# Hybrid decoder layer in seven-product blocks: last block's differences, a left-over product, two row loads and some copies moved in the order

## The chip, the cores and the metric

The kernel runs on one core of a Trainium2 chip. The metric is the device time of one launch in microseconds (us), as the median of several runs. The core has five engines that run side by side and wait for each other by semaphores: TensorE (PE, matrix products, with PEld for loading its weights), VectorE (DVE, elementwise work), ScalarE (ACT, activations and copies), GpSimd (POOL) and SyncE (SP, which issues most DMA transfers). Each engine works off its own instructions strictly in the order in which the program lists them.

## The reference

```python
xn = rms_norm(h, ln_g)
proj = jnp.einsum('bsd,de->bse', xn, w_in)
b_gate, c_gate, x_conv, g_conv, x_lru, g_lru = jnp.split(proj, splits, axis=-1)
y_conv = b_gate * causal_depthwise_conv(c_gate * x_conv, conv_w)
y_conv = headwise_rms_norm(y_conv, 8, conv_out_g) * jax.nn.silu(g_conv)
y_lru = rg_lru_mixer(x_lru, lru_conv_w, ...)
y_lru = headwise_rms_norm(y_lru, 16, lru_out_g) * jax.nn.silu(g_lru)
y = jnp.concatenate([y_conv, y_lru], axis=-1)
h = h + jnp.einsum('bse,ed->bsd', y, w_out)
return rms_norm(h, final_g)
```

All is float32, with 2048 positions, a model width of 1024 and an input projection to 6144 columns. `rg_lru_mixer` is a width-4 convolution `u`, two gates (sigmoids of small block-diagonal products of `u`) and a linear recurrence over positions. Nearly all arithmetic is in the two large projections.

## The kernel before

**The steps.** The program is a list of 64 steps (`steps`, L268 to L272), written out in an order that is fixed by hand; no scheduler changes it. Steps 0 to 23 compute the input projection for the first 1024 positions, one step for each 256 columns: kind `l` (`lru`, L707), `a` (`conv_a`, L821) and `b` (`conv_b`, L857) in turn. Steps 24 to 47 do the same for the second 1024 positions. Steps 48 to 55 and 56 to 63 are the output projection (kind `o`, `outp`, L884).

**A step.** A step multiplies a 2x2 set of weight blocks (the stationary side, tiles `s`) with a 2x2 set of activation blocks (`T`, tiles `th` and `tl`). From step 3 on it does so with seven block products instead of eight: products 0 to 6 use sums and differences of the blocks, and their results are added up in four PSUM banks A to D. Each operand is split into a rounded high part and the rest (`th` and `tl`; the two halves of an `s` tile), so a product is 4 blocks x 3 matmuls of 128x512, 12 in all (`mm`, L1009). Sums, splits and copies lie on DVE (line 163 for all elementwise additions and differences), ACT (casts to the high part at L213 for weights, L451, L1160 and L1221 for activations) and POOL.

**The order within a step.** A step runs through slots (loop at L1261). Usually these are products 0, then product 6 of the step before (left over from it), 1, 3, 2, 4, 5. Bank A gathers products 0, 1, 2 and 5, and after each of the first three ACT copies the partial sum out (`q1` at L1315, `u2` at L1318, `rr` at L1321); the next product on bank A must wait until that copy has read it. Those copies are named `q`, `u` or `rr` in the profile, whichever tile they alternate to: line L1318 is always the copy after product 1, L1321 the one after product 2. Bank B may take product 6 only when the combination before (`xx`, `ob`, `gb` or `gl` from the bank, by `put(22, ...)`) has read it.

**Helpers.** `at(k, f)` runs `f` at the k-th `tick`, that is, k slots later. `prep(n, s)` is a step's piece of preparation: from step 3 to 23 it forms and splits weight tiles (`s_plan`, L192: `hi(i)` is ACT's cast, `lo(i)` the rest on DVE or POOL), later it loads ready tiles from DRAM (`s_loads`, L236). `defer` holds a function back while `held[0]` is a list, and `release` runs what was held.

**Changes of the activation set.** The activations change at steps 24, 48 and 56. These steps open the new set with eight products on what is ready (L1240), the next one (25, 49, 57) is `late` and runs products 0, 4, 5, 1, 3, 2 (`AFTER`, L233); their product 6 comes in the step after. A `Change` object loads, subtracts and splits the new blocks in numbered slots: `of_x` (L478) for the positions, `of_w` (L500) for the output weights, `cut` (L447) for casts and low parts.

**The plain start.** Steps 0 to 2 use eight plain products, and beside them the differences of the activation blocks are formed: `bit(j)` (L1155) has four pieces for block j, `do_bits(n)` runs the next n, and `after1` (L1194) and `after2` (L1213) call it in the eight slots of steps 1 and 2. The gates of step 0 (`gates`, L743: four matmuls at L751 into two PSUM tiles; `sigs`, L754: four sigmoids at L758) are due in the slots of step 2. There are two such PSUM tiles, so the second pair of gates waits for the sigmoids of the first.

**Output rows.** The second half of the output projection needs rows that an earlier step left in DRAM (`od`), loaded by `load` (L891) into `xr`, and added at L942 (`ob<-ob,xr`). SP issues its transfers one after the other, the loads of `s`, `tl`, `raw` and `zr` among them.

## Time and profile before

| what | value |
|---|---|
| median of three runs | 1316.51 us (1314.1 to 1317.4) |
| the profiled execution's own time | 1314.92 us |
| its span | 1313.1 us |
| busy: PE, PEld, DVE, ACT, POOL | 1289.5, 1061.0, 1046.0, 748.7, 250.0 us |
| mean granted clock of PE | 0.996 |
| DMA | 355.29 MB, mean 271 GB/s |

The span lies between the first and the last instruction of the profiled execution; its own time is 1.8 us longer. A row in order of time has the start in the span, the duration, engine, line, operation and `out<-in`; `[3.41 <-ACT i L758]` means that the engine idled 3.41 us before it until ACT's operation on `i` at line 758 was done. A row of stretches has the stretch, its length, busy time and number of instructions of each engine, the granted clock of PE as a share of full speed, the share of time in which the DMA engines were busy, and GB/s.

### The profile page before, as it was taken

What the parts mean: (1) busy time and instruction counts of PE and PEld (TensorE: products, weight loads), DVE (VectorE), ACT (ScalarE), POOL (GpSimd) and SP (SyncE); (2) the same over time, 40 slices, a digit from 0 to 9 for tenths busy, and PEclk for the clock granted to TensorE, in tenths of its full rate; (3) what the DMA queues carried; (4) which work ended last, traced back from release to release, by engine and by line L of the source; (5) the groups of instructions that cost most, each with busy time, mean ns of one, the idle gap of its engine ahead of it and who ended that gap; (6) DMA issues with size and microseconds to landing.
All of it is one profiled execution on the core that took longest, in us unless ns stands there. A gap on an engine that the chain in (4) does not pass through costs nothing.

```text
span 1313.1 us, 16711 instructions
## 1 busy us (share of the span) xinstructions
PE 1289.5 (98%) x5688; PEld 1061.0 (81%) x5688; DVE 1046.0 (80%) x1284; ACT 748.7 (57%) x1141; POOL 250.0 (19%) x189
## 2 busy tenths in 40 slices
PE   7989999999999999999999999999999999999997
PEld 6867888888888888778888888888888888887886
DVE  6789898999999998967666666667559767649886
ACT  7576767576675667566454645454466433445443
POOL 3204243344435441001010110101011000000000
PEclk9989999999999999999999999999999999999999
DMA  7128887898989887651899999999789986697654
GB/s 294 32 90 290 290 286 264 302 350 283 345 302 329 295 301 280 207 199 33 277 318 296 340 352 333 324 355 362 236 271 339 260 261 229 249 402 273 235 179 160
DMA packets 157958, 355.29 MB, mean 271 GB/s; under 512 B 16944, under 2 KB 51760, under 8 KB 157872
## 3 DMA queue, kind: packets, MB, share of 16 engines
q1 hardware_dynamic: 153264, 338.17, 74.4%
q0 software_dynamic: 4320, 15.73, 3.1%
q8 instruction: 45, 0.74, 0.2%
q14 instruction: 41, 0.34, 0.1%
q10 hardware_dynamic: 288, 0.32, 0.1%
HBM read 217.11 MB, written 137.04 MB: 270 GB/s over the span
## 4 chain that ended last, share of the span: by engine, by line
PE 82%; DVE 8%; DMA 5%; ACT 3%; issue 2%; SPq 0%; POOL 0%; ACTq 0%; DVEq 0%
PE bank L1014 79%; DMA s<-so 2%; DVE tl L163 2%; PE gate L751 2%; DVE traw L163 1%; DMA tl<-td 1%; DMA zr<-rsd 1%; DMA xr<-od 1%; DMA fg<-in_final_g_dram 1%; DVE u L723 1%; ACT i L758 0%; DVE s L163 0%; ACT r L758 0%; ACT th L451 0%; PE tp L554 0%
## 5 line engine op out<-in xcount | busy, mean ns | idle before, releaser
L1014 PE MATMUL bank<-th,s 128*128 128x512 f32 x3632 | 1129.6, 390 | 5.7 <-ACT rr L1318 1.6
L1014 PEld LDWEIGHTS bank<-th,s 128*128 128x128 f32 x3632 | 682.7, 188 | 151.7 <-ACT rr L1318 2.5
L1014 PE MATMUL bank<-tl,s 128*128 128x512 f32 x1816 | 708.2, 390 | 1.8 <-DVE tl L163 1.6
L1014 PEld LDWEIGHTS bank<-tl,s 128*128 128x128 f32 x1816 | 341.4, 188 | 74.5 <-DVE tl L163 3.0
L163 POOL TENSOR_TENSOR s<-raw,s 128x512 fp32r<-128x512 f32 x62 | 115.1, 1870 | 231.1 <-ACT s L213 176.0
L213 ACT CAST s<-raw 128x512 fp32r<-128x512 f32 x140 | 85.4, 618 | 48.4 <-PE bank L1014 32.8
L163 POOL TENSOR_TENSOR gb<-gb,sg 128x1024 f32<-128x1024 f32 x16 | 43.4, 2712 | 335.5 <-ACT sg L682 335.5
L163 DVE TENSOR_TENSOR s<-raw,s 128x512 fp32r<-128x512 f32 (+1 forms) x125 | 91.6, 755 | 10.6 <-ACT s L1073 6.7
L163 DVE TENSOR_TENSOR s<-s,s 128x512 fp32r<-128x512 f32 x105 | 86.6, 824 | 2.1 <-ACT s L213 1.5
L163 DVE TENSOR_TENSOR tl<-traw,th 128x512 fp32r<-128x512 f32 x85 | 60.8, 748 | 19.4 <-ACT th L451 13.4
L213 ACT CAST s<-s 128x512 fp32r<-128x512 f32 x105 | 64.7, 616 | 4.3 <-DVE s L163 4.0
L723 DVE SCALAR_TENSOR_TENSOR u<-xl,pt,u 128x1024 f32<-128x1024 f32 x48 | 61.3, 1278 | 6.1 <-ACT u L719 5.5
L835 DVE SCALAR_TENSOR_TENSOR t<-p,pt,t 128x1024 f32<-128x1024 f32 x32 | 46.5, 1454 | 16.6 <-ACT t L832 15.8
L1315 ACT COPY q<-bank 128x512 f32<-128x512 f32 x58 | 33.9, 584 | 40.9 <-PE bank L1014 31.5
L163 DVE TENSOR_TENSOR st<-u,st 64x512 fp32r<-64x512 f32 x64 | 53.8, 841 | 2.0
L758 ACT ACTIVATE r<-gate,pt 64x512 f32<-64x512 f32 x64 | 43.7, 683 | 17.3 <-PE gate L751 16.5
L1318 ACT COPY rr<-bank 128x512 f32<-128x512 f32 x31 | 18.1, 584 | 53.6 <-PE bank L1014 53.3
L1318 ACT COPY u<-bank 128x512 f32<-128x512 f32 x27 | 15.8, 585 | 52.4 <-PE bank L1014 52.4
L163 DVE TENSOR_TENSOR traw<-traw 128x512 f32<-128x512 f32 x60 | 41.8, 701 | 4.7 <-DMA traw<-in_w_out_dram 3.6
L451 ACT CAST th<-traw 128x512 fp32r<-128x512 f32 x64 | 36.1, 618 | 16.1 <-DVE traw L163 14.2
L758 ACT ACTIVATE i<-gate,pt 64x512 f32<-64x512 f32 x64 | 43.8, 684 | 1.1
L1321 ACT COPY u<-bank 128x512 f32<-128x512 f32 x31 | 18.1, 585 | 43.6 <-PE bank L1014 43.5
(169 smaller groups left out, 1294.1 us busy)
## 6 DMA issues: line engine op xcount, KB each, us to landing
sd<-s SPq DMA_DIRECT2D x151, 512.0 KB
s<-sd SPq DMA_DIRECT2D x151, 512.0 KB
raw<-in_w_in_dram SPq DMA_DIRECT2D x104, 256.0 KB
raw<-yd SPq DMA_DIRECT2D x64, 256.0 KB
traw<-in_w_out_dram SPq DMA_DIRECT2D x64, 256.0 KB
so<-so SPq DMA_DIRECT2D x22, 512.0 KB
s<-so SPq DMA_DIRECT2D x22, 512.0 KB
yd<-gl SPq DMA_DIRECT2D x32, 256.0 KB
```

What stands on the lines that cost most here:

```text
L163: (eng or nc.vector).tensor_tensor(out=out, in0=a, in1=b, op=op)
L213: nc.scalar.copy(dst[i][0], val(i))
L451: nc.scalar.copy(self.dst[i, j][0], self.r[i, j])
L723: nc.vector.scalar_tensor_tensor(out=v["u"], in0=o1[:, 1 + j:1 + j + N2], scalar=lw[j], in1=v["u"], op0=ALU.mult, op1=ALU.add)
L751: nc.tensor.matmul(ps[j], v["gw"][n][:, j, :], v["st"][j][:, sl], start=(n == 0), stop=(n == 1))
L758: nc.scalar.activation(out=g_[hi, sl], in_=v["ps"][j][src], func=AF.Sigmoid, bias=pt[src, bias + k:bias + k + 1])
L835: nc.vector.scalar_tensor_tensor(out=tcur["t"], in0=p[:, 2 + j:2 + j + N2], scalar=cw[j], in1=tcur["t"], op0=ALU.mult, op1=ALU.add)
L1014: nc.tensor.matmul(bank, a[:, js], b, start=start and n == 0, stop=stop and n == 2, skip_group_check=more)
L1315: nc.scalar.copy(q1, bk["A"])
L1318: nc.scalar.copy(u2, bk["A"])
L1321: nc.scalar.copy(rr, bk["A"])
```

## The change

The edits are small, and each moves instructions; no operation is added or left out.

- Steps 1 and 2: the last four pieces of `bits`, block 3, go from the last two slots of step 1 into the first four slots of step 2, one each.
- Steps 3 to 23, and the later ones that form their weight tiles themselves: `hi(5)` is deferred, and `held[0]` is opened in the slot of product 0, so that ACT's cast of this weight tile (`s2` or `s`) stands behind the copy `q1`.
- Step 25 and 26, at the change of positions: `sixth` does its four subtractions in one slot and the four casts and low parts in the next; step 26 runs products 0, 3, left-over 6, 1, 2, 4, 5; and the scaling `m1` of `conv_a` is held back there until the copy `u2`.
- Steps 49 and 57 (the `late` ones of the output projection): the casts of `Change` in the slot of product 1 come behind the copy `u2`, and the preparation of the next step in the slot of product 2 behind the copy `rr` and the two combinations that use it.
- Step 56: the two row loads three slots sooner.

```diff
-                lambda: hi(5),
+                lambda: defer(lambda: hi(5)),
...
-        def sixth(self, *js):
-            for j in js:
+        def sixth(self):
+            for j in range(NB):
                 tt(self.r[6, j], self.r[6, j], self.r[1, j], ALU.subtract)
-            self.cut([(6, j) for j in js])
+            at(1, lambda: self.cut([(6, j) for j in range(NB)]))
...
-                self.sixth(0, 1)
-                at(1, lambda: self.sixth(2, 3))
+                self.sixth()
...
-                at(1, m1)
+                at(1, lambda: defer(m1))
...
-            at(5, lambda: load(0))
-            at(6, lambda: load(1))
+            sooner = 3 if ph == 1 and m == 2 else 0
+            at(5 - sooner, lambda: load(0))
+            at(6 - sooner, lambda: load(1))
...
-            do_bits(2)
+            if s < 6:
+                do_bits(2)
...
         def after2(s):
-            do_bits(2)
+            do_bits(1)
...
             slots = (0, 6) + ORDER[1:] if not late else AFTER
+            if kind != "o" and n > 1 and opens(n - 2):
+                slots = (0, 3, 6, 1, 2, 4, 5)
...
+                if i == 1 and slots[2] == 6:
+                    held[0] = []
                 tick()
...
                 if late:
-                    change.slot(16 + s)
+                    if i != 1 or kind != "o":
+                        change.slot(16 + s)
...
                 elif s == 0:
+                    held[0] = []
                     prep(n, 6)
...
-                    held[0] = [] if i == 2 else None
-                    prep(n + 1, s - 1)
+                    if i == 2 and not late:
+                        held[0] = []
+                    if i != 2 or kind != "o" or not late:
+                        prep(n + 1, s - 1)
...
-                if s == 1 and not late:
+                if i == 6 and not late and s < 3:
...
                 if i == 0:
                     q1 = sm_q1[0] = sm("q1")
                     nc.scalar.copy(q1, bk["A"])
+                    release()
                 elif i == 1:
                     u2 = sm_u2[0] = sm(("u2", "rr")[n % 2])
                     nc.scalar.copy(u2, bk["A"])
+                    release()
+                    if late and kind == "o":
+                        change.slot(16 + s)
...
                     if late:
                         put(12, bk["D"], rr)
+                        if kind == "o":
+                            prep(n + 1, s - 1)
```

What this does to the engines' orders is shown at three places. A row there is a line of the program it is from (the lines of the changed kernel differ by one or more from those of the profile), the operation, `out<-in` and the size.

On ACT at the border of steps 1 and 2, before (`th<-traw` are the casts of the activation blocks, `s<-raw` of a weight tile, `xx` and `p` copies of PSUM banks, `r` and `i` the sigmoids of step 0's gates):

```order
L1160 CAST th<-traw 128x512
L814 COPY xx<-bank 128x512
L814 COPY p<-bank 128x512
L1160 CAST th<-traw 128x512
L1073 CAST s<-raw 128x512
L1160 CAST th<-traw 128x512
L814 COPY xx<-bank 128x512
L758 ACTIVATE r<-gate,pt 64x512
L758 ACTIVATE i<-gate,pt 64x512
L758 ACTIVATE r<-gate,pt 64x512
L758 ACTIVATE i<-gate,pt 64x512
L832 ACTIVATE t<-p,pt 128x1024
```

And the same place on ACT in the changed kernel:

```order
L1160 CAST th<-traw 128x512
L813 COPY xx<-bank 128x512
L813 COPY p<-bank 128x512
L1073 CAST s<-raw 128x512
L813 COPY xx<-bank 128x512
L757 ACTIVATE r<-gate,pt 64x512
L757 ACTIVATE i<-gate,pt 64x512
L757 ACTIVATE r<-gate,pt 64x512
L757 ACTIVATE i<-gate,pt 64x512
L831 ACTIVATE t<-p,pt 128x1024
L839 COPY hp<-p 128x2
L1160 CAST th<-traw 128x512
```

Two casts have left the place between the copies; the first of them now stands behind `t`, the second behind the four sigmoids that follow it. On DVE the six operations of block 3 have moved along: one goes ahead of the two multiply-adds `t<-p,pt,t` of step 1, five behind them.

On ACT in steps 25 and 26, before (`th<-traw` are the casts of the four blocks for product 6, `u_5065` is the copy `rr` of step 25, `q_5099` and `u_5149` the copies `q1` and `u2` of step 26):

```order
L451 CAST th<-traw 128x512 x2
L1321 COPY u_5065<-bank 128x512
L451 CAST th<-traw 128x512 x2
L1315 COPY q_5099<-bank 128x512
L758 ACTIVATE r<-gate,pt 64x512
L758 ACTIVATE i<-gate,pt 64x512
L758 ACTIVATE r<-gate,pt 64x512
L758 ACTIVATE i<-gate,pt 64x512
L620 CAST rt<-sums 128x512
L832 ACTIVATE t<-p,pt 128x1024
L1318 COPY u_5149<-bank 128x512
```

And the same place on ACT in the changed kernel:

```order
L1334 COPY u_5059<-bank 128x512
L451 CAST th<-traw 128x512 x4
L1324 COPY q_5099<-bank 128x512
L757 ACTIVATE r<-gate,pt 64x512
L757 ACTIVATE i<-gate,pt 64x512
L757 ACTIVATE r<-gate,pt 64x512
L757 ACTIVATE i<-gate,pt 64x512
L619 CAST rt<-sums 128x512
L757 ACTIVATE r<-gate,pt 64x512
L757 ACTIVATE i<-gate,pt 64x512
L757 ACTIVATE r<-gate,pt 64x512
L757 ACTIVATE i<-gate,pt 64x512
```

The copy `rr` of step 25 stands ahead of all four casts, the second group of sigmoids has come forward, and the copy `u2` and the scaling `t` follow behind this piece. On DVE all four differences come ahead of `xx<-bank,u`, and the four low parts behind it. On PE the order of products is 0, 3, 6, 1, 2 instead of 0, 6, 1, 3, 2; the four gate matmuls and the small products of `norm_ps` (L627) keep their slots.

On SP in step 56, before (`fg` are the final gains, `td` the stored differences of the output weights, `od` the rows):

```order
L889 DMA fg<-in_final_g_dram 128x1024
L239 DMA s<-so_125 128x1024
L518 DMA tl<-td_130 128x512
L518 DMA tl<-td_131 128x512
L518 DMA tl<-td_132 128x512
L518 DMA tl<-td_133 128x512
L239 DMA s<-so_125 128x1024
L894 DMA xr<-od_138 128x1024
L239 DMA s<-so_125 128x1024
L307 DMA raw<-yd_86 128x512 x2
L297 DMA zr<-rsd_89 128x1024
```

And the same place on SP in the changed kernel:

```order
L888 DMA fg<-in_final_g_dram 128x1024
L239 DMA s<-so_125 128x1024
L893 DMA xr<-od_138 128x1024
L517 DMA tl<-td_130 128x512
L517 DMA tl<-td_131 128x512
L517 DMA tl<-td_132 128x512
L517 DMA tl<-td_133 128x512
L893 DMA xr<-od_139 128x1024
L239 DMA s<-so_125 128x1024 x2
L307 DMA raw<-yd_86 128x512 x2
L297 DMA zr<-rsd_89 128x1024
```

The first row load has passed four `tl` transfers and one `s`; the second, which stood behind both pairs of `raw` and their `zr`, has passed two `s`, four `raw` and two `zr`.

## The prediction

> **What bounds the kernel now.** I read the page first, then the waits of PE, then PE, ACT and DVE in order of time around each wait. The page says that TensorE (PE) has almost no idle time:
>
> ```profile
> PE 1289.5 (98%) x5688; PEld 1061.0 (81%) x5688; DVE 1046.0 (80%) x1284; ACT 748.7 (57%) x1141; POOL 250.0 (19%) x189
> ```
>
> So the change can only win where PE idles or its clock is low. The stretches of the span (after the span of time: its length, then busy time and instruction count of PE, PEld, DVE, ACT and POOL, the granted clock, DMA share, GB/s) say what kind of place that is:
>
> ```profile
> 50.00:100.00 50.00, 46.31 (x188) 36.68 (x187) 42.44 (x57) 33.56 (x50) 4.48 (x5) 0.93 0.19 66
> 380.20:436.90 56.70, 56.70 (x252) 46.89 (x250) 54.59 (x56) 37.42 (x55) 24.82 (x15) 1.00 0.91 313
> 550.00:650.00 100.00, 97.44 (x428) 79.44 (x427) 71.77 (x85) 60.00 (x82) 9.62 (x5) 1.00 0.49 160
> ```
>
> The second row is one cycle of three steps in the middle: PE has no gap, 252 matmuls in 56.70 us, 0.225 us each, which I use below as the pace of PE at full clock. A product of 12 matmuls is 2.7 us. Nothing that only touches such a cycle can gain. The first and the third hold gaps, and the first a lower clock. The waits of PE over the whole span (sum, times, longest) give the list:
>
> ```profile
> PE gate L751 <- ACT i L758: 3.6, 2, 3.4
> PE bank L1014 <- ACT rr L1318: 1.6, 2, 1.3
> PE bank L1014 <- DVE xx L163: 1.3, 1, 1.3
> PE bank L1014 <- DVE ob L163: 1.1, 1, 1.1
> PE norm_ps L627 <- ACT i L758: 0.8, 1, 0.8
> ```
>
> These five are the four places that the edits touch: the second plain step, step 26, step 49, and steps 57 and 58. Other waits of PE (the start, the end, `q1` in step 3) keep their instruction order.
>
> **Part 1: the last block's differences out of the second plain step.** PE, in order of time (start, duration, in brackets the idle time and what ended it):
>
> ```profile
> 73.25 0.39 PE L1014 MATMUL bank<-th,s 128*128 128x512 f32 x1
> 77.05 0.79 PE L751 MATMUL gate<-st,bh 128*128 128x512 f32 x1 [3.41 <-ACT i L758]
> 78.45 0.79 PE L751 MATMUL gate<-st,bh 128*128 128x512 f32 x1 [0.18 <-ACT i L758]
> 79.47 0.63 PE L1014 MATMUL bank<-th,s 128*128 128x512 f32 x1
> 83.74 0.41 PE L1014 MATMUL bank<-tl,s 128*128 128x512 f32 x1
> ```
>
> The second pair of gate matmuls needs the PSUM tiles of the first pair, which ACT's four sigmoids read. ACT was late:
>
> ```profile
> 70.56 0.59 ACT L814 COPY p<-bank 128x512 f32<-128x512 f32 x1
> 73.17 0.62 ACT L1160 CAST th<-traw 128x512 fp32r<-128x512 f32 x1 [2.02 <-DVE traw L163]
> 74.62 0.62 ACT L1160 CAST th<-traw 128x512 fp32r<-128x512 f32 x1 [0.31 <-DVE traw L163]
> 75.62 0.68 ACT L758 ACTIVATE r<-gate,pt 64x512 f32<-64x512 f32 x1
> ```
>
> Two casts of the last block waited for its differences on DVE, and the sigmoids stood behind them. In the new order both casts stand behind the sigmoids. ACT goes on from 70.56: 0.5 for the copy of `p`, 0.5 for the cast of `s`, 0.5 for the copy of `xx`, so the first sigmoid starts at 72.1 instead of 75.62. From that sigmoid to the gate matmuls it was 1.43 us to the first pair (77.05) and 2.83 to the second (78.45); so they may start at 73.5 and 74.9. PE gets there at 73.5: the 3.41 us are gone, and about 0.8 is left before the second pair. The clock:
>
> ```profile
> 78.00:80.00 2.00, 1.82 (x5) 1.26 (x5) 0.39 (x1) 1.98 (x4) 0.00 (x0) 0.50 0.03 8
> ```
>
> It was 0.50 after the 3.41 us of idling, and the ten matmul intervals from 79.47 to 83.74 took 4.27 us instead of 2.25. The longest idle times elsewhere in the steady program, 1.3 us in the list above, stand in rows with a clock of 1.00, so I take it that 0.8 us leaves the clock alone. Then the second pair starts 3.57 us earlier, the 1.02 us from there to 79.47 become about 0.55 (half the time, rounded up), and the 4.27 become 2.25: 3.57 + 0.47 + 2.02 = **6.1 us**. Bounds: 3.6 if the clock falls all the same, 6.9 if the 0.8 us goes too.
>
> The Trainium skill ("TensorE: Matmul & The Clock Gate", section "A second HAM failure mode: psum-queue depth-cycling") speaks against this: short idle times between groups of matmuls, each far below the window, can be enough to make the clock fall again and again. By it this part gains 3.6 and the whole sum is 2.5 us smaller. The rows with 1.00 around waits of 1.3 us are against it here.
>
> What takes the place: DVE. Of its six moved operations five now follow its pair of multiply-adds, which started at 79.61 when ACT's `t` was ready and now start some 3.5 us earlier:
>
> ```profile
> 79.60:100.80 21.20, 18.12 (x25) 0.90 0.47 171
> 100.09 0.69 DVE L163 TENSOR_TENSOR tl<-t,th 128x512 fp32r<-128x512 f32 x1
> 101.47 0.50 PE L1014 MATMUL bank<-th,s 128*128 128x512 f32 x1 [0.73 <-ACT q L1315]
> ```
>
> From 76.1, with 18.1 us of work and five or six more operations of 0.65 (row 100.09 has 0.69), DVE is through with the last low part at 98.1, only 2.7 us earlier than 100.8, while PE comes 6.1 earlier. So DVE loses 3.4 us of its lead on PE. The low parts of `T[3]` are first read in the product after the one at 101.47, 2.7 us on, so the lead was more than that; I cost the lag at nothing and keep up to 2.7 us as its upper end. The 0.73 us for `q1` stays: in step 3 there is no left-over product between product 0 and product 1.
>
> **Part 2: step 26 and the deferred `m1`.**
>
> ```profile
> 555.48 0.50 PE L1014 MATMUL bank<-th,s 128*128 128x512 f32 x1 [1.32 <-DVE xx L163]
> 557.33 0.50 PE L1014 MATMUL bank<-th,s 128*128 128x512 f32 x1 [0.19 <-ACT th L451]
> 566.70 0.71 PE L627 MATMUL norm_ps<-rt,sel 128*96 128x256 f32 x4 [0.82 <-ACT i L758]
> 567.25 0.39 PE L1014 MATMUL bank<-th,s 128*128 128x512 f32 x1
> 554.01 0.58 ACT L1321 COPY u<-bank 128x512 f32<-128x512 f32 x1
> ```
>
> The left-over product waits for `xx`, which waits for the copy `u`, queued behind two casts on ACT that wait for DVE. Now the casts follow the copy and all four differences stand ahead of `xx`; product 3 runs 2.7 us between. Two differences take the place of two low parts ahead of `xx`, so DVE has it at 555.4 as before, and PE needs it at 556.7. The four low parts behind it end at about 556.4 to 558.3 (0.6 apart, as two of DVE's operations take 1.28 in row 1190.77 below) and are read from 556.9 on, three matmuls (0.68) apart: covered by 0.5 us. The last gate matmul ahead of the wait starts at 555.48 less 1.32 less its own 0.40, 553.76, and PE is free 0.2 later. From there to 567.25 are 13.3 us; three products (8.1), four gate matmuls (0.9) and `norm_ps` (567.25 less 566.70, 0.55) are 9.6, so 3.7 are waits. What comes new: products 1 and 2 follow each other on bank A with the copy between them. A bare copy costs PE 0.9 us (row 101.47: 0.73 and the ramp); 0.55 of it lies under `norm_ps`, some 0.4 us stay. I take **3.3 us**; bounds 2.4 (the copy late by an ACT operation and a half) and 3.7.
>
> **Part 3: step 49.** Two casts move behind the copy that PE waits for.
>
> ```profile
> 1028.02 0.50 PE L1014 MATMUL bank<-th,s 128*128 128x512 f32 x1 [0.33 <-ACT rr L1318]
> ```
>
> The copy comes 1.0 us earlier, two casts of 0.5: the wait goes, with the matmul latency around it **0.6 us** (0.3 to 0.7). The casts are read two products later.
>
> **Part 4: steps 56 to 58, the rows sooner.**
>
> ```profile
> 1161.09 0.32 SPq L894 DMA_DIRECT2D xr<-od  x1
> 1162.36 0.32 SPq L239 DMA_DIRECT2D s<-so  x1
> 1172.86 1.29 DVE L163 TENSOR_TENSOR raw<-raw,zr 128x512 f32<-128x512 f32 x2 [0.29 <-DMA zr<-rsd]
> 1177.08 1.22 DVE L163 TENSOR_TENSOR ob<-ob,xr 128x1024 f32<-128x1024 f32 x1 [2.93 <-DMA xr<-od]
> 1182.74 0.69 DVE L163 TENSOR_TENSOR s<-s,raw 128x512 f32<-128x512 f32 x1
> 1184.05 0.58 ACT L1318 COPY rr<-bank 128x512 f32<-128x512 f32 x1
> 1184.68 0.50 PE L1014 MATMUL bank<-th,s 128*128 128x512 f32 x1 [1.30 <-ACT rr L1318]
> 1190.77 1.28 DVE L163 TENSOR_TENSOR ob<-bank,u 128x512 f32<-128x512 f32 x2
> 1191.51 0.50 PE L1014 MATMUL bank<-th,s 128*128 128x512 f32 x1 [1.05 <-DVE ob L163]
> ```
>
> DVE waits 2.93 us for the second row; what is behind it releases a cast on ACT and the copy that PE needs. With both rows ahead, the next to come last is `zr`. SP passes one 512 KB transfer per 1.27 us here (the two SP rows), and one transfer more is now ahead of `zr`: 1174.1 instead of 1172.86, two multiplications, and `ob` starts at 1175.4, 1.7 us earlier. The copy had ended at 1184.63 and ends at 1182.9 then. PE is free at 1183.2 (1184.68 less the wait and a ramp of 0.2): the wait of 1.30 goes, 1.6 with the ramps. For the left-over product of step 57, DVE reaches `ob<-bank,u` 1.7 us earlier and 1.2 more since two operations now follow it: done at 1188.5 (1190.77 + 0.68 - 2.9), where PE comes after two products at 1183.2 + 5.4 = 1188.6: 1.05 and its ramps, 1.3, go. Together 2.9, less 0.2 for leads this thin: **2.7 us** (1.3 to 2.9). The `s` and `tl` transfers that the rows pass come 1.3 to 2.6 us later; PE's list above names no DMA among its waits, so I cost that at nothing; without that cover it would be up to 2.6 us, the second rival's size.
>
> **Costed at nothing:** the swap of `hi(5)` behind `q1` in the steps between. The cast of 0.62 us moves past a copy; DVE idles 56.70 less 54.59, 2.1 us a cycle, and three casts are 1.9. Without that cover see the third rival.
>
> **The sum:** 6.1 + 3.3 + 0.6 + 2.7 = 12.7 us. The profiled execution took 1314.92 us, its span 1313.1: 1302.2. The median of the three runs, 1316.51, lies 1.6 above it, so I forecast 1303.8 for a median.
>
> **The rivals.** *First: PE catches DVE, or the clock falls.* In step 3 PE waits up to 2.7 us for low parts, or part 1 gains 3.6 instead of 6.1. For: DVE is the busiest engine there after PE. Time: 1303.8 + 2.6 = 1306.4. *Second: the end is not mended*, as the 0.2 to 0.4 us of lead in part 4 are too thin: 1303.8 + 2.7 = 1306.5. *Third, the other side: DVE becomes the bound in the seven cycles of steps 3 to 23.* The three later casts use up 1.9 of its 2.1 us; if they also shift its operations into POOL's, an operation can take this:
>
> ```profile
> 106.67 2.89 DVE L163 TENSOR_TENSOR s<-raw,s 128x512 fp32r<-128x512 f32 x1
> ```
>
> That is 2.2 more than the 0.69 of its kind. With two more such collisions a cycle: 1.9 + 4.4 - 2.1 = 4.2 us by 7, 29 us, 1333; it decides from one a cycle on, 2.0 by 7 = 14 us, which eats the gain. Against: from 150 to 520 DVE waits for PE's banks five times, so it is through in time:
>
> ```profile
> DVE xx L163 <- PE bank L1014: 4.0, 5, 1.0
> ```
>
> By the Trainium skill ("GPSIMD Engine Reference", section "Specifications") VectorE and GpSimd share their SBUF interfaces, and an operation with two SBUF inputs is one of those that suffer. The 2.89 us agree. *Fourth: the DMA gives it back.* Loads bind the stretch from 700 on and do not come earlier, so PE waits for them: 9.4 of the gains lost, 1313.2. Against: in the row from 550 the DMA share is 0.49, so its queue drains there and moves with PE.
>
> **Chances.** Forecast 0.60 (its own range 1301 to 1306), first rival 0.20, second 0.08, fourth 0.05, third 0.04, and 0.03 for more than I count. A measurement of this kernel can tell about 0.3%, 4 us, from no change: the forecast, the first two rivals and the rest are faster, 0.91; the fourth is the same, 0.05; the third slower, 0.04. The range takes in the low end of the forecast and the first two with 2 us: 1300.5 to 1308.5.
>
> **What would show it.** Right: no wait of the gate matmuls over 1 us near 73, a clock of 1.00 from 50 to 100, PE at the 101.47 matmul near 95.3; no `xx` wait in step 26 and a small one for `u2` behind `norm_ps`; no wait for `rr` in steps 49 and 57 nor for `ob` in step 58. Wrong: a clock of 0.50 near 77, new waits of PE in steps 3 to 23, or the sum of PE's gaps less than 9 us smaller.

## The result

The changed kernel takes 1304.99 us (median of 6 runs, 1303.76 to 1307.17) where the kernel before takes 1316.18 (6 runs, 1314.1 to 1317.4). The ratio is 0.9918, with a 95% interval of 0.9906 to 0.9931: about 10.8 us less, 9.1 to 12.4. The profiled execution of the changed kernel took 1304.39 us, its span is 1302.6: 10.5 us less than before in both. The 12.7 us that the prediction added up are just above the interval of the gain.

TensorE's line of the page, the stretches that stood in the prediction (the cycle in the middle comes 5.1 us earlier now), and the waits of TensorE that are new or answer to those listed for before:

```profile
PE 1285.2 (99%) x5688; PEld 1059.1 (81%) x5688; DVE 1042.7 (80%) x1284; ACT 748.1 (57%) x1141; POOL 247.7 (19%) x189
```

```profile
50.00:100.00 50.00, 48.57 (x210) 38.80 (x210) 45.18 (x61) 37.69 (x56) 5.55 (x6) 1.00 0.23 84
375.10:431.80 56.70, 56.70 (x252) 46.89 (x251) 54.05 (x57) 37.39 (x55) 24.35 (x15) 1.00 0.91 312
550.00:650.00 100.00, 99.76 (x441) 82.34 (x440) 73.24 (x87) 60.91 (x83) 9.66 (x5) 1.00 0.51 171
```

```profile
PE bank L1014 <- ACT u L1334: 1.2, 1, 1.2
PE bank L1014 <- ACT q L1324: 0.7, 1, 0.7
PE gate L750 <- ACT i L757: 0.7, 1, 0.7
PE bank L1014 <- ACT rr L1328: 0.5, 1, 0.5
PE bank L1014 <- ACT u L1328: 0.2, 1, 0.2
```

The clock is 1.00 in the first stretch (0.93 before), the waits for `xx` and `ob` are gone, and the first line of the list is new. (Line numbers differ a little: L758 of before is L757 here, and the copies of L1315, L1318 and L1321 are L1324, L1328 and L1334.) To add the places up, I took from the trace every distance between the starts of two matmuls that follow each other, and of those over 0.3 us what goes beyond 0.225. This holds the waits, their ramps (the wider distances of the first matmuls after a wait) and the half clock; I call it TensorE's excess. It is counted from one profile of each kernel. In us:

| place | before | after | gain | forecast |
|---|---|---|---|---|
| gates near 73, clock | 7.66 | 1.60 | 6.1 | 6.1 |
| steps 3 and 4 (90 to 140) | 1.00 | 2.48 | -1.5 | 0 |
| step 26 | 3.56 | 0.41 | 3.15 | 3.3 |
| step 49 | 0.60 | 0.74 | -0.1 | 0.6 |
| steps 57 and 58 | 2.91 | 0.66 | 2.25 | 2.7 |
| start (to 50) | 7.33 | 7.27 | 0.1 | 0 |
| other places | 0.42 | 0 | 0.4 | 0 |
| all | 23.49 | 13.16 | 10.3 | 12.7 |

The spans differ by 0.2 us more than the places, and 0.5 us of the sum (the start and the other places) is not where the edits are.

**The gates.** TensorE and then ScalarE of the changed kernel, in order of time:

```profile
73.07 0.50 PE L750 MATMUL gate<-st,bh 128*128 128x512 f32 x1
74.47 0.50 PE L750 MATMUL gate<-st,bh 128*128 128x512 f32 x1 [0.67 <-ACT i L757]
75.05 0.39 PE L1014 MATMUL bank<-th,s 128*128 128x512 f32 x1
```

```profile
71.16 0.60 ACT L813 COPY xx<-bank 128x512 f32<-128x512 f32 x1
71.64 0.69 ACT L757 ACTIVATE r<-gate,pt 64x512 f32<-64x512 f32 x1
75.59 0.62 ACT L1160 CAST th<-traw 128x512 fp32r<-128x512 f32 x1
```

The sigmoid follows the copy of `xx` at once, the cast stands behind the sigmoids, and the first pair of gate matmuls waits for nothing. The next product starts 0.58 us after the second pair.

**Step 3.** The new wait, on TensorE, and what ScalarE, VectorE and GpSimd did ahead of it:

```profile
107.31 0.50 PE L1014 MATMUL bank<-th,s 128*128 128x512 f32 x1 [1.17 <-ACT u L1334]
```

```profile
105.12 0.62 ACT L213 CAST s<-s 128x512 fp32r<-128x512 f32 x1 [2.48 <-DVE s L163]
105.64 1.05 ACT L572 ACTIVATE xrow<-xrow 128x1024 f32<-128x1024 f32 x1
106.69 0.57 ACT L1334 COPY u<-bank 128x512 f32<-128x512 f32 x1
```

```profile
97.10 2.28 DVE L784 TENSOR_TENSOR_SCAN r<-r,u 128x1024 f32<-128x1024 f32 x1
99.49 2.06 DVE L663 SCALAR_TENSOR_TENSOR gl<-r,pt,gl 128x1024 f32<-128x1024 f32 x1
101.47 2.89 DVE L163 TENSOR_TENSOR s<-raw 128x512 f32<-128x512 f32 x1
104.39 0.69 DVE L163 TENSOR_TENSOR s<-s,raw 128x512 f32<-128x512 f32 x1
```

```profile
98.92 1.55 POOL L163 TENSOR_TENSOR s<-raw,s 128x512 fp32r<-128x512 f32 x1 [20.46 <-ACT s L213]
100.43 3.38 POOL L163 TENSOR_TENSOR gb<-gb,sg 128x1024 f32<-128x1024 f32 x1
```

TensorE needs the bank that ScalarE copies into `u`. The copy stands in ScalarE's queue behind a cast of step 4's `s`, and this cast waits for VectorE's sum of 104.39. VectorE is late: its scan (97.10) starts 2.13 us behind TensorE's product that waits for `q` (94.97). Before, it started 0.77 us ahead of it (100.70 against 101.47):

```profile
100.70 2.29 DVE L785 TENSOR_TENSOR_SCAN r<-r,u 128x1024 f32<-128x1024 f32 x1
```

So 2.9 us of lead are gone, and two operations beside GpSimd's take 2.06 and 2.89 us.

**Step 26, and step 57.** TensorE in step 26; VectorE in step 57:

```profile
558.00 0.64 PE L626 MATMUL norm_ps<-rt,sel 128*96 128x256 f32 x4
558.88 0.50 PE L1014 MATMUL bank<-th,s 128*128 128x512 f32 x1 [0.24 <-ACT u L1328]
```

```profile
1166.18 1.29 DVE L163 TENSOR_TENSOR raw<-raw,zr 128x512 f32<-128x512 f32 x2 [5.11 <-DMA zr<-rsd]
1167.39 1.22 DVE L163 TENSOR_TENSOR ob<-ob,xr 128x1024 f32<-128x1024 f32 x1
```

The bare copy between products 1 and 2 leaves 0.24 us behind `norm_ps`. In step 57 `ob` no longer waits for a row; the last that it stands behind is `zr`.

**Step 49.** ScalarE, then TensorE:

```profile
1016.04 0.62 ACT L451 CAST th<-tl 128x512 fp32r<-128x512 f32 x1 [7.69 <-DMA tl<-td]
1017.38 0.62 ACT L451 CAST th<-tl 128x512 fp32r<-128x512 f32 x1 [0.73 <-DMA tl<-td]
1018.96 0.58 ACT L1328 COPY rr<-bank 128x512 f32<-128x512 f32 x1
```

```profile
1019.58 0.50 PE L1014 MATMUL bank<-th,s 128*128 128x512 f32 x1 [0.47 <-ACT rr L1328]
```

Two of the four casts do stand behind the copy now, but the other two wait for staged blocks that the DMA queue brings, the second until 1017.38.

### The profile page after: what moved, and what is told of

Its sections match the earlier page's. It is cut to its first block, busy times and chain, and to the rows that moved or that the text cites. A ratio compares the mean times of both kernels' runs of the same rounds, so it can differ in the third digit from the quotient of the medians.

```text
span 1302.6 us, 16692 instructions
## 1 busy us (share of the span) xinstructions
PE 1285.2 (99%) x5688; PEld 1059.1 (81%) x5688; DVE 1042.7 (80%) x1284; ACT 748.1 (57%) x1141; POOL 247.7 (19%) x189
## 4 chain that ended last, share of the span: by engine, by line
PE 84%; DMA 4%; DVE 3%; ACT 2%; issue 1%; SPq 0%; DVEq 0%; ACTq 0%
PE bank L1014 82%; PE gate L750 2%; DMA s<-so 2%; DMA tl<-td 1%; DMA zr<-rsd 1%; DVE s L163 1%; DMA raw<-yd 1%; DVE tl L163 0%; DVE ob L163 0%; DVE r L784 0%; ACT th L451 0%; ACT L769 0%; ACT r L769 0%; DVE u L163 0%; DVE raw L163 0%
## 5 line engine op out<-in xcount | busy, mean ns | idle before, releaser
L163 DVE TENSOR_TENSOR s<-raw,s 128x512 fp32r<-128x512 f32 (+1 forms) x125 | 88.3, 729 | 10.6 <-ACT s L1073 6.7
L1324 ACT COPY q<-bank 128x512 f32<-128x512 f32 x58 | 33.9, 585 | 50.2 <-PE bank L1014 48.5
L757 ACT ACTIVATE r<-gate,pt 64x512 f32<-64x512 f32 x64 | 43.7, 683 | 17.8 <-PE gate L750 17.0
L1328 ACT COPY rr<-bank 128x512 f32<-128x512 f32 x31 | 18.1, 584 | 51.1 <-PE bank L1014 51.0
L163 DVE TENSOR_TENSOR raw<-raw,zr 128x512 f32<-128x512 f32 x64 | 41.1, 683 | 7.6 <-DMA zr<-rsd 7.5
L1328 ACT COPY u<-bank 128x512 f32<-128x512 f32 x27 | 15.8, 585 | 52.2 <-PE bank L1014 51.7
L1334 ACT COPY u<-bank 128x512 f32<-128x512 f32 x31 | 18.1, 584 | 47.0 <-PE bank L1014 46.9
L757 ACT ACTIVATE i<-gate,pt 64x512 f32<-64x512 f32 x64 | 43.8, 684 | 1.1
```

What stands on the lines that cost most here:

```text
L163: (eng or nc.vector).tensor_tensor(out=out, in0=a, in1=b, op=op)
L757: nc.scalar.activation(out=g_[hi, sl], in_=v["ps"][j][src], func=AF.Sigmoid, bias=pt[src, bias + k:bias + k + 1])
L1324: nc.scalar.copy(q1, bk["A"])
L1328: nc.scalar.copy(u2, bk["A"])
L1334: nc.scalar.copy(rr, bk["A"])
```

## The experiments

The theory: the four places of the forecast pay separately, and what is missing has two causes: VectorE's lost lead, which TensorE meets in step 3 through ScalarE's queue, and the landing of the staged blocks in step 49. The main rival: the new wait comes from the cast of `hi(5)` that now stands behind `q1`, and the rest is a matter of single profiles. All times below are ratios to the kernel before on the same chip, with 95% intervals.

**Part 1 alone**, in the kernel before:

```diff
-            do_bits(2)
+            if s < 6:
+                do_bits(2)
...
         def after2(s):
-            do_bits(2)
+            do_bits(1)
```

> The kernel before with part 1 alone (the last block's differences later). Theory: the gates and the clock are worth 6.1 us, and because VectorE keeps only part of its lead, the copy u in step 3 stands behind a cast that waits for VectorE and behind a square, so 1.4 us come back there: 4.7 us less than before, about 1311.5, with a wait of TensorE of 1.0 to 1.3 us for ACT's u in step 3, and the waits of steps 26, 49, 57 and 58 as before. Rival: the new wait in step 3 comes from the cast of hi(5), which the full change puts behind q1: then part 1 alone shows no u wait in step 3 and gains 6.1, about 1310.

Measured: 0.997 (0.9959 to 0.9981), 3.9 us less than 1315.26 (2.5 to 5.4). TensorE's wait in step 3 is there, without any change to `hi(5)`:

```profile
107.25 0.50 PE L1014 MATMUL bank<-th,s 128*128 128x512 f32 x1 [1.02 <-ACT u L1322]
```

Beyond the pace of 0.225 us there are 1.61 us at the gates and 2.50 in steps 3 and 4, as in the changed kernel. The rival falls. The 3.9 us and the 1.5 that come back in step 3 make 5.4, somewhat less than the 6.1 of the table.

**Step 26 alone**, in the kernel before: the methods `sixth` and `of_x`, the line of `m1`, the order 0, 3, 6, 1, 2 and the release behind `u2`, as in the diff of the change.

> The kernel before with the reordered step 26 alone (products 0, 3, sixth, 1, 2, the four differences together, m1 and the casts behind the copy). Theory: 3.3 us less than before, about 1313: the waits of 1.3 and 0.2 us in step 26 go and some 0.4 stay between products 1 and 2. Rival: it only pays together with part 1, or the loads of the output stage take it back: within 1 us of before.

Measured: 0.9974 (0.9964 to 0.9984), 3.4 us less (2.1 to 4.7); step 26 keeps 0.41 us. The theory holds. Its profiled execution also has a wait near 720 that no edit touches; TensorE, and a stretch behind it:

```profile
719.89 0.50 PE L1013 MATMUL bank<-th,s 128*128 128x512 f32 x1 [2.19 <-DMA s<-sd]
```

```profile
722.00:724.00 2.00, 2.00 (x6) 1.56 (x5) 0.00 (x0) 0.00 (x0) 0.00 (x0) 0.50 1.13 390
```

**The rows sooner, alone**, in the kernel before:

```diff
-            at(5, lambda: load(0))
-            at(6, lambda: load(1))
+            sooner = 3 if ph == 1 and m == 2 else 0
+            at(5 - sooner, lambda: load(0))
+            at(6 - sooner, lambda: load(1))
```

> The kernel before with only the two output rows of step 56 loaded three slots sooner. Theory: VectorE's wait of 2.9 us for the second row goes, so the rr wait of 1.3 us in step 57 shrinks to 0.2 or less, but the ob wait of step 58 stays at 0.7 to 1.1 us: 1.5 us less than before. Rival: the rows carry the whole of part 4: both waits go, 2.3 to 2.9 us less. Second rival: the transfers that the rows pass are missed, and TensorE shows a new DMA wait there: no gain.

Measured: 0.9987 (0.9978 to 0.9996), 1.7 us less (0.5 to 2.9). In the trace the excess ahead of the `rr` product of step 57 falls from 1.47 to 0.28, and the wait for `ob` in step 58 stays at 1.07. The theory holds; there is no new DMA wait near the passed transfers. Near 720 this profile too has a wait, a shorter one, and the clock stays:

```profile
721.30 0.50 PE L1015 MATMUL bank<-th,s 128*128 128x512 f32 x1 [1.27 <-DMA s<-sd]
```

```profile
722.00:724.00 2.00, 2.00 (x11) 1.64 (x10) 1.17 (x2) 1.69 (x2) 0.00 (x0) 1.00 1.04 379
```

**Copies first, alone**, in the kernel before (steps 49 and 57):

```diff
                 if late:
-                    change.slot(16 + s)
+                    if i != 1 or kind != "o":
+                        change.slot(16 + s)
...
                     nc.scalar.copy(u2, bk["A"])
+                    if late and kind == "o":
+                        change.slot(16 + s)
...
                         put(12, bk["D"], rr)
+                        if kind == "o":
+                            prep(n + 1, s - 1)
```

> The kernel before with only the casts, differences and low parts of steps 49 and 57 put behind the copies and partial sums. Theory (step 49's wait of after is due to the tl transfers, which did not come earlier in step with TensorE): here nothing ahead is faster, the transfers land as early against TensorE as before, and the 0.6 us of step 49 go; the ob wait of step 58 goes too (1.05 us and its ramp), the rr wait of step 57 stays at 1.2 to 1.4: 1.8 us less than before. Rival: the order of the casts has nothing to do with step 49's wait: it stays at 0.3 to 0.6 us here as well, 1.2 us less.

Measured: 0.9988 (0.998 to 0.9997), 1.6 us less (0.4 to 2.6). The wait of step 49 is gone altogether, so is that for `ob`. The wait for `rr` in step 57 is 0.78 us, where 1.2 to 1.4 were expected and 1.30 stood before; its product starts 7.6 us behind the `ob` operation that waits for the row in both, so the row came sooner against TensorE, which this edit does not explain. The trace fits the theory for step 49, but does not show by itself that the order did it: the fourth staged block landed early here (1.03 us in the count of the table further down, at which the old order would not have waited either). The four parts measured alone sum to 10.6 us, against 10.8 for the whole.

**The swap of `hi(5)` alone**, in the kernel before:

```diff
-                lambda: hi(5),
+                lambda: defer(lambda: hi(5)),
...
                 elif s == 0:
+                    held[0] = []
                     prep(n, 6)
...
                     nc.scalar.copy(q1, bk["A"])
+                    release()
```

> The kernel before with only the cast of hi(5) behind the copy q1 in the steps of the cycles. Theory: it moves nothing that TensorE waits for: the same time within 0.1% (1.3 us), no new wait of TensorE from 150 to 520. Rival (VectorE becomes the bound in the seven cycles): from 1.5 us slower on, with waits of TensorE in steps 3 to 23. Second rival: it is a part of the gain: over 1 us faster.

Measured: 1.0006 (0.9997 to 1.0014), and no wait of TensorE from 150 to 520. It costs nothing that this measurement can tell, as forecast.

**Half of part 1**, in the changed kernel:

```diff
-            if s < 6:
+            if s < 7:
                 do_bits(2)
```

> The changed kernel, but the last slot but one of the second plain step keeps its pair of differences and one cast (only the last slot's pair is moved). Theory: one cast stands ahead of the sigmoids and waits for VectorE again, so TensorE waits 1.0 to 2.0 us before the first gates instead of 0; the clock stays at 1.00 afterwards; VectorE comes 1.3 us less late to step 3, so the u wait of 1.2 us there goes to 0.3 or less: about even with the changed kernel (within 1 us). Rival (short idle times are enough for the clock to fall): a granted clock of 0.50 behind the gates and 2 us more than the changed kernel.

Measured: 0.994 (0.9928 to 0.9953), 2.9 and 3.7 us more than the changed kernel in its two measurements (0.9918 and 0.9912); I had expected within 1. The wait in step 3 is gone (0.95 us in steps 3 and 4, as before), but the cast that stays makes TensorE wait 2.49 us where 1.0 to 2.0 were expected, and the clock falls: the rival came true. TensorE, and the stretch behind the gates:

```profile
77.19 0.50 PE L750 MATMUL gate<-st,bh 128*128 128x512 f32 x1 [2.49 <-ACT i L757]
```

```profile
78.00:80.00 2.00, 1.41 (x3) 1.16 (x4) 0.26 (x1) 1.98 (x4) 0.00 (x0) 0.53 0.03 8
```

**The square behind the copy**, in the changed kernel:

```diff
-            at(3, lambda: nc.scalar.activation(out=t, in_=t, func=AF.Square, accum_out=ss[:, b:b + 1]))
+            at(3 + (c == b == 0), lambda: nc.scalar.activation(out=t, in_=t, func=AF.Square, accum_out=ss[:, b:b + 1]))
```

> The changed kernel with ScalarE's first sum of squares (the instruction of 1.05 us ahead of the copy u in step 3) one slot later. Theory: TensorE waits for u in step 3 because ScalarE passes a late cast and then this square before it copies; with the square behind, u ends 1.2 us sooner and the wait falls from 1.2 to 0.2 us or less: 1.1 us less than the changed kernel. Rival (VectorE's lag itself is the bound): the wait moves to the next product or the next partial sum and the time is the same.

Measured: 0.9922 (0.9908 to 0.9935), the time of the changed kernel. Three waits of TensorE stand where one was:

```profile
106.50 0.50 PE L1014 MATMUL bank<-th,s 128*128 128x512 f32 x1 [0.17 <-ACT u L1334]
115.44 0.50 PE L1014 MATMUL bank<-th,s 128*128 128x512 f32 x1 [0.48 <-ACT q L1324]
130.20 0.47 PE L750 MATMUL gate<-st,bh 128*128 128x512 f32 x1 [0.40 <-DVE st L163]
```

Together with the wait for `q` in step 3 they make 2.79 us against 2.48. My theory that the square is what has to go falls; the rival holds: VectorE's lag is the bound, and it comes out at the next place.

**The staged blocks one slot sooner**, in the changed kernel:

```diff
-            if q in (6, 7, 9, 15):
-                self.place((3, 1, 2, 6)[(6, 7, 9, 15).index(q)])
+            if q in (6, 7, 9, 14):
+                self.place((3, 1, 2, 6)[(6, 7, 9, 14).index(q)])
```

> The changed kernel with the four staged blocks of the sixth product in steps 48 and 56 ordered one slot sooner, so ahead of one 512 KB transfer of s. Theory (step 49's wait comes from ScalarE's casts waiting for these blocks): they land 1.3 us sooner and the wait of 0.5 us for rr in step 49 goes: 0.7 us less than the changed kernel. Rival: the wait has another cause on ScalarE or VectorE and stays at 0.5. Second rival: the passed transfer of s is missed, and TensorE or ScalarE waits for it: no gain or slower.

Measured: 0.9923 (0.9909 to 0.9937). In the trace step 49 waits for nothing, and steps 57 and 58 have 0.30 us in place of 0.66. A difference of 1 us is smaller than the interval, and this trace alone does not show the theory: the changed kernel itself waits for nothing in step 49 in its second profile, which comes next.

**The changed kernel, profiled once more:**

> The changed kernel itself, profiled once more. Theory: what TensorE waits for in steps 3 and 26 and at the gates is the same to 0.05 us, while step 49's wait is a matter of when the second staged block lands: the wait is that landing, counted from the first of the norm_ps matmuls, less 0.95 us (0.63 at 1.58, 0.98 at 1.93, none at 0.80 so far). Rival: step 49's wait is fixed by the order and shows 0.5 to 0.7 us again wherever the block lands.

Measured: 0.9912 (0.9898 to 0.9925). Gates, step 3 and step 26 are the same to 0.02 us (1.60, 2.47, 0.41); step 49 waits for nothing. ScalarE there:

```profile
1015.78 1.31 ACT L451 CAST th<-tl 128x512 fp32r<-128x512 f32 x2 [7.03 <-DMA tl<-td]
1018.03 0.58 ACT L1328 COPY rr<-bank 128x512 f32<-128x512 f32 x1
```

The two casts follow each other here. The table shows, in us, when the block that the copy stands behind has landed by the trace, counted from the start of the first of the `norm_ps` matmuls ahead of the wait, and TensorE's excess at the product behind the copy (without the 0.11 us of the matmul after it, which the first table holds too):

| casts ahead of the copy | kernels | landing | excess |
|---|---|---|---|
| four (fourth block) | before; part 1; step 26; rows; swap | 1.76; 2.19; 2.15; 1.67; 2.49 | 0.49; 0.94; 0.89; 0.43; 1.23 |
| two (second block) | changed; again; half; square; copies first | 1.58; 0.26; 1.93; 0.80; -0.32 | 0.63; 0; 0.98; 0; 0 |

The excess is the landing less 1.26 us in the first row, and the landing less 0.95, or nothing, in the second. The theory holds: the order fixes what the copy waits for, and the landing fixes how long. The queue's order around these blocks is the same in all ten, and the landing moves by 0.8 us (first row) and 2.2 (second). Some of that is chance from one execution to the next: the changed kernel itself stands at 1.58 and at 0.26. Whether the blocks also come later because TensorE is earlier can't be told from these. In the kernel with the blocks one slot sooner and the three further down that are built on it, the second block landed at -0.89, 0.10, -0.50 and -1.03, and none of the four waits in step 49. That is what the theory of the sooner blocks expects.

**Four low parts on GpSimd**, in the kernel with the blocks sooner:

```diff
-                    low(v, T[i, j])
+                    low(v, T[i, j], g if i == 6 else None)
```

> The changed kernel with the staged blocks one slot sooner, and with four of the eight low parts that VectorE makes in the third plain step (those of the sixth left matrix, first read in step 4) made by GpSimd. Theory (VectorE's lag behind the six later differences is what TensorE meets in step 3): VectorE has 4 operations of 0.6 us less, 2.4 us, which is the lag of 2.9 us but for 0.5; the u wait of step 3 falls from 1.2 to 0.3 us or less, no new wait at q in step 3 and at the gates of step 4, and step 49 shows none either: 1.5 to 2 us less than the changed kernel. Rival: GpSimd's four operations run beside VectorE's and stretch them (an operation of 0.69 us took 2.89 beside one of GpSimd's), so that VectorE gains less than it gives: the u wait stays at 1 us or grows, and the time is that of the changed kernel or more.

Measured: 0.9932 (0.9918 to 0.9945). The wait for `u` grew to 2.02 us. The rival holds; VectorE and GpSimd:

```profile
101.86 1.78 DVE L163 TENSOR_TENSOR s<-raw 128x512 f32<-128x512 f32 x1
103.67 2.77 DVE L163 TENSOR_TENSOR s<-s,raw 128x512 f32<-128x512 f32 x1
```

```profile
100.84 2.25 POOL L163 TENSOR_TENSOR s<-raw,s 128x512 fp32r<-128x512 f32 x1
103.05 2.85 POOL L163 TENSOR_TENSOR gb<-gb,sg 128x1024 f32<-128x1024 f32 x1
```

GpSimd's added work pushes its two operations onto the sums that the cast waits for.

**The last block's four differences in VectorE's idle time**, and, apart from it, **step 4's low parts on VectorE instead of GpSimd**, both with the blocks sooner. In the first, the differences stand together ahead of the two multiply-adds and the casts stay behind the sigmoids:

```diff
         def after2(s):
-            do_bits(1)
+            if s == 0:
+                b11, b12, b21, b22 = (tr[3][n] for n in range(4))
+                tt(b11, b12, b11, ALU.subtract)
+                tt(b12, b22, b12, ALU.subtract)
+                tt(b22, b22, b11, ALU.subtract)
+                last(3)
...
```

```diff
-        g = nc.gpsimd if PLAIN < n < 3 * KT else None
+        g = nc.gpsimd if PLAIN + 1 < n < 3 * KT else None
```

> The changed kernel with the staged blocks one slot sooner, and with the last block's four differences on VectorE together ahead of its two multiply-adds of the third plain step, where it idles 1.7 us for ScalarE's t; the casts and low parts stay where the change put them, behind the sigmoids. Theory (TensorE's u wait in step 3 is VectorE's lag): three operations of 0.6 us move into the idle time, VectorE is 1.7 us less late, the gates keep their 0 and 0.8 us and the clock 1.00, and the u wait of 1.2 us falls to 0.2 or less with no new wait behind it (the square alone, in the other run, moved it to q and to the next gates): 1.3 us less in step 3 and 0.5 less in step 49 than the changed kernel, about 1302.5. Rival: the collision with GpSimd falls on other operations of VectorE and the wait stays at 0.8 us or more.

> The changed kernel with the staged blocks one slot sooner, and with the three low parts of step 4's left matrices that GpSimd makes in step 3 made by VectorE. Theory: two of VectorE's operations took 0.8 and 2.2 us more beside GpSimd's there; without the first of GpSimd's operations its product of gb and sg starts 1.5 us sooner and still runs beside VectorE's, so about half of the 3 us is saved, and VectorE pays 0.6 us for each of three operations behind: the u wait falls from 1.2 to 0.5 us or less, and a wait of up to 1 us may come in step 4. Rival: the stretched operation is not GpSimd's doing, or the collision just moves with gb: the u wait stays at 1 us or more.

Measured: 0.9917 (0.9904 to 0.9931) and 0.9908 (0.9894 to 0.9921). In the first, the wait for `u` is 0.44 us: the three operations fill the idle time, but VectorE's scan starts 1.22 us behind the product that waits for `q` (97.07 against 95.85), so only 0.9 of the 1.7 us came through, and part of the wait stays: more than the theory's 0.2, less than the rival's 0.8. In the second the wait for this `u` is no longer in the list of waits, and nothing new stands in step 4: the theory holds. VectorE and GpSimd of the second:

```profile
99.80 3.16 DVE L663 SCALAR_TENSOR_TENSOR gl<-r,pt,gl 128x1024 f32<-128x1024 f32 x1
102.89 0.68 DVE L163 TENSOR_TENSOR s<-raw 128x512 f32<-128x512 f32 x1
103.60 0.69 DVE L163 TENSOR_TENSOR s<-s,raw 128x512 f32<-128x512 f32 x1
```

```profile
98.17 3.71 POOL L163 TENSOR_TENSOR gb<-gb,sg 128x1024 f32<-128x1024 f32 x1 [19.39 <-ACT sg L681]
```

GpSimd is through at 101.9 and `s<-raw` takes 0.68 instead of 2.89. VectorE's scan is as late as in the changed kernel (97.41 against TensorE's 95.25), so the wait of step 3 needs both: the lost lead, and the collision that falls on the operations ahead of the cast. From 50 us on, the excess of TensorE in these two profiles is 4.0 and 4.5 us, against 4.8 with the sooner blocks alone and 5.9 and 5.3 in the two profiles of the changed kernel; the intervals of the times overlap, so neither is shown to be faster than the change. By the Trainium skill ("GPSIMD Engine Reference", section "Specifications") VectorE's operations with two SBUF inputs contend with GpSimd; the 2.89 and 0.68 us of `s<-raw`, with and without GpSimd beside it, agree.

## Why the prediction was right, and where it was off

The forecast of 1303.8 us is 1.2 below the median of 1304.99. Its sum of 12.7 us stands against 10.5 in the profiled spans; the misses by place, with the 0.5 us gained where no edit is, add up to that but for 0.2. One of the prediction's own signs of being wrong came, a new wait in steps 3 to 23, and so did a rest of the wait for `rr` in step 49.

- **Part 1** was worth 6.1 us, as worked out. ScalarE's sigmoid came at 71.64 and the gates at 73.07 and 74.47 (forecast 72.1, 73.5 and 74.9; TensorE was already 0.4 us earlier at the gates of 66.79, now 66.39). The clock stayed at 1.00 with 0.67 us of waiting left. That it is exactly 6.1 is in part luck: over the five profiles with the old order here (before, step 26, rows, copies first, swap) the excess at the gates is 6.80 to 7.66 us, and the profile from which the 6.1 was worked out has the most; against the other four the gain is 5.2 to 6.0. The rule of the Trainium skill that was weighed against it ("TensorE: Matmul & The Clock Gate", "A second HAM failure mode: psum-queue depth-cycling") did not show: with it 2.5 us would be missing here.
- **VectorE's lag** is the step that failed. The forecast had VectorE lose 3.4 us of its lead; it lost 2.9. But the text looked for the reader of that lead at TensorE alone ("The low parts of `T[3]` are first read in the product after the one at 101.47 ... I cost the lag at nothing"). TensorE does not wait for these low parts. It waits for a copy on ScalarE behind a cast that needs VectorE. That is 1.5 us, inside the 2.7 kept as the upper end, and is the first rival in its mechanism of VectorE's lead, though not by the low parts named there. Part 1 alone, the half of it and the last two kernels show it.
- **Part 2** was right: 3.15 us for 3.3, and the 0.4 that should stay stayed (0.41).
- **Part 3** was right in its size but not in its premise. The copy does come two casts earlier, but "the wait goes" held the landing of the staged blocks fixed. In the profile of after, the fourth block landed at 2.91 us: by the first row of the table the old order would have waited 1.65, and 0.63 are left, so the edit gained 1.0 there. The -0.1 in the first table hangs on the profile: the second one of the changed kernel has no wait there, which would be a gain of 0.6. Over the five profiles of each row the mean excess is 0.80 and 0.32 us, 0.5 less, though these are different kernels. The wait is set by when a transfer lands, which a single profile of before can't tell.
- **Part 4** gave 2.25 for 2.7. The last thing that VectorE waits for is `zr`, as said, and `ob` starts 9.7 us earlier than before; TensorE is 8.5 earlier there (1174.53 against 1182.99), so 1.2 us were gained where 1.7 were forecast. The thin leads of 0.2 us counted at the end of that part were not there. The rows and the later copies each pay alone (1.7 and 1.6 us, the latter with step 49), and mend different waits: with the rows alone `rr` falls to 0.12 us and `ob` stays, with the copies alone `ob` goes and 0.78 of `rr` stays.
- **The swap of `hi(5)`** costs nothing, and the third rival (VectorE as the bound of the cycles) did not come: the cycle in the middle has TensorE busy for 56.70 of 56.70 us. The fourth (the DMA takes it back) did not come: TensorE is 8.5 us earlier at step 57, and whether the 0.7 us of step 49 have to do with that is open.

## What to carry to other kernels

When an edit lets TensorE run ahead, follow the engine that keeps its old time to every queue that reads from it: here VectorE's lag reached TensorE not by its operands but by a cast in front of a copy on ScalarE. A wait that hangs on a transfer is a distribution, not a number: profile the kernel before twice before you count on the last tenths of it. And an engine's idle time ahead of a wait (VectorE's 1.7 us here) is where moved work should go first.

## What was not expected of the hardware

- The clock fell after TensorE idled 2.49 us (half of part 1) and 2.19 us (near 720 in one profile): 0.53 and 0.50 in the stretches of 2 us quoted. Behind 1.27 us (near 720 in another) and 1.32 us (step 26 before) it stayed at 1.00. The length of one idle time does not decide, though: in the start, TensorE of the changed kernel idled 2.07 us until 8.43 and that of the copies-first kernel 2.18 us until 8.41, and the clock stayed at 1.00. By the clock's records in the traces, all its changes within one profile lie whole multiples of 3.413 us apart, in all 14 profiles. With the span cut into such stretches, from 50 us on the clock fell behind every stretch at full clock in which TensorE was busy for 41% or less, and behind none with 51% or more. In the start this does not separate: 48% passed, and 60% did not. The Trainium skill ("TensorE: Matmul & The Clock Gate", "What's actually happening") has the clock fall after an idle window of about 3.4 us; the 3.413 us agree, but here the window need not be idle throughout.
- After the same wait of 3.4 us for the gates, what is left of the excess at the gates without the first gap, most of it half clock, is 4.1 us in the profile of before (7.66 less 3.58) and 3.2 in that of step 26 alone (6.80 less 3.58), where nothing differs up to there: the price of one wait varies by 0.9 us from one execution to the next. The low clock lasted two such stretches in the first (76.94 to 83.77) and one in the second (79.04 to 82.45).
- A VectorE operation that met GpSimd's was held up rather than slowed by a factor. In the rows above, VectorE's 128x512 operations end 0.5 to 0.6 us after the GpSimd operation that they met: 104.36 against 103.81 in the changed kernel, 106.44 against 105.90 with the four low parts on GpSimd. The 128x1024 operation `gl` ends 1.08 after it (102.96 against 101.88, with step 4's low parts on VectorE). They look as if most of their work began when GpSimd's was done. So what such a meeting costs is about what is left of GpSimd's operation. This was read from the traces and not tried by itself.
- The same transfers near 712 to 722 made TensorE wait 0 to 2.2 us in different profiles of kernels that are the same up to there or nearly so; with the start (5.2 to 8.0 us of excess) this may be what spreads the times of one kernel by some us. That was not tried by itself.
